# Hybrid neighbourhood-attention layer on one core: another order of the last first-group products, and a place for silu's table load

## The chip, the cores and the metric

One core of a Trainium2 chip runs the whole layer. The metric is the device time of one execution, in microseconds. Before the change it is 590.04 us, the median of 3 runs (589.38 to 590.24).

## What is computed

One layer of a diffusion backbone on 1024 tokens (a grid of 16 rows by 64 columns) of width 1024, with 256 context tokens. Cut to what matters:

```
h  = rmsnorm(x, norm_g) * (1 + scale) + shift          # scale, shift, gate = silu(c) @ w_ada + b_ada
hc = rmsnorm(ctx, norm_g) * (1 + scale_c) + shift_c
q, k, v, za, u, bg, cg, zc = split(h @ w_in)           # 8 parts of 512 columns
kc, vc = split(hc @ w_in[:, 512:1536])
attn = neighbourhood_attention(norm(q), norm(k), v, norm(kc), vc, rpb) * silu(za)
conv = bg * conv3(cg * u) * silu(zc)
out  = x + gate * (concat(attn, conv) @ w_out)
```

All is float32. The kernel splits each operand of a large product into a high and a low part and adds three products: high by high, high by low, low by high.

## The kernel before

The program has four stages. Times in brackets are where they lie in the profile.

**First stage (0 to 63 us).** A list of words, `STEPS` (L37 to L49), sets the order in which the instructions are written; an engine runs its instructions in the order in which they are written, and a wait at one holds all that stand behind it. The stage makes `h` for eight blocks of 128 features, `h0` to `h7`, and at the same time the first group of 384 projected columns: u, bg and cg of the first conv group. That group has six PSUM banks: `acc00`, `acc10`, `acc20` for the first half of the tokens (u, bg, cg) and `acc01`, `acc11`, `acc21` for the second half. A word `fcHKI` (L665) is three products of half H, feature block K: I = 0 is high by high, 1 the weights' low part by `h`'s high part, 2 the weights' high part by `h`'s low part. `qhK` and `qlK` (L673, L679) make the high part (ScalarE) and the low part (VectorE) of the weights of the *next* 384 columns, the tile `w`, out of `wr`, which a DMA has loaded. `conv0` (L756) takes one step of `conv_group(0)` (L409): the first such step copies the first half's u from its bank to `ub` (ScalarE, `keep`, L416) and multiplies it with cg in its bank into `cu` (VectorE, `multiplied`, L420); the second step does the same for the second half. `Rt2` transposes and `R2` copies the context's row scales (`rs2<-tr`). `rg1` to `rg3` are three VectorE products for the rotary table.

**Second stage (63 to about 250 us).** The first pools of PSUM are closed and others opened over the same banks. 32 token tiles are projected (`proj_tile`, L307): each is one PSUM tile `pacc`, 8 feature blocks of 3 products. Its first tile lies in the bank that held `acc00`, its second in that of `acc20`. The products of block K need `w`'s high part K, and from the second on its low part K.

**Third stage (250 to 508 us).** 36 calls of `quarter(n)` (L1022) do the attention, with the exponentials on ScalarE. Between its pieces stand filler products (`pu`), the units of 128 columns of the gates and of the conv groups. A unit has two halves, each with a `pu` tile of its own, and there are two such tiles, so a unit's first half waits until the tile of the unit before it has been read. The last two units are the conv gate zc (read by `silus`, L500: silu out of PSUM into `zs`) and bg. Quarter 34 has the last exponentials. ScalarE needs another function table for silu than for exp; an `ACT_TABLE_LOAD` is put ahead of the first instruction that needs another table than the one loaded.

**Fourth stage (508 us to the end).** The output projection, seven blocked products into `pout` tiles, their scaling and addition, and the stores.

Of the kernel before, what the change touches and what calls it, by code (L numbers as in the profile page):

```python
# [13 lines left out]
AF = mybir.ActivationFunctionType  # L14
# [34 lines left out]
]  # L49
CONTEXT = "Hi0 Hi1 Lo0 Lo1 Hi2 Hi3 Lo2 Lo3 Hi4 Hi5 Lo4 Lo5 Hi6 Hi7 Lo6 Lo7"  # L50

# [4 lines left out]
def body(tc, es, x, xb, xt, cb_, ct, w_mod, w_gate, b_ada, w_grp, w_col, q_g, k_g, bias, w_out, vecs, cst, out):  # L56
# [21 lines left out]
    pe, act, dve, pool = every = [ordered(e) for e in (nc.tensor, nc.scalar, nc.vector, nc.gpsimd)]  # L78
# [49 lines left out]
    few = cp.tile([P, 8], F32, name="few")  # L128
# [5 lines left out]
    ones = oner[:, 0:1]  # L134
# [196 lines left out]
    def do_acts():  # L331
        for c in soon + (slow if not any(c[1] and c[1].__name__ == "product" for c in soon) else []):
            if c[0]:
                c[0]()
                c[0] = None

    def do_frees(most):
        while most > 0 and slow and slow[0][2] is not None and not slow[0][0]:
            slow.pop(0)[1]()
            most -= 1  # L340
        return most

    def do_dves(most=99):
        most = do_frees(most)
        for queue in chores:
            while queue and not queue[0][0] and (queue is soon or most > 0 and not soon):
                on_dve = queue.pop(0)[1]
                if on_dve:
                    on_dve()
                    most -= 1  # L350
# [612 lines left out]
    def pair_of(n):  # L963

        h, g = divmod(n, 4)
        return [(a, heads[h], 2 * g + a) for a in range(2)] if 0 <= h < NH else []

    def both(v, n, part=slice(0, 31)):

        lo, hi = span(2 * (n % 4))  # L970
        return v[:, :, part.start * 12:min(part.stop, hi - lo) * 12]

    def maxima_of(n):

        lo, hi = span(2 * (n % 4))
        v = mg[:]
        return bass.AP(v.tensor, v.offset + lo * 16, [list(v.ap)[0], [4, 2], [16, hi - lo], [1, 12]])
# [6 lines left out]
    def maxima(e):  # L984

        blocks = turned(e) if e < 4 * NH else []
        nb = len(blocks)
        if not blocks:
            return None
        pm = psm.tile([P, 512], F32, name="pmx", tag="C", bufs=2)  # L990
        for i, b in enumerate(blocks):
            pe.transpose(pm[:, i * P:(i + 1) * P], mx[:, b * P:(b + 1) * P], ident)
        rm = ap.tile([P, 2], F32, name="rm", tag="rm", bufs=8)
        dve.tensor_reduce(rm[:, :nb], pm[:, :nb * P].rearrange("p (i k) -> p i k", i=nb), AX.X, ALU.max)

        def back():
            for i in range(nb):
                pe.transpose(pm[:, 256 + i * P:256 + (i + 1) * P], rm[:, i:i + 1].broadcast_to([P, P]), ident)
            v, step = mg[:, blocks[0] * P:], (blocks[-1] - blocks[0]) * P or P
            act.copy(bass.AP(v.tensor, v.offset, [list(v.ap)[0], [step, nb], [1, P]]),  # L1000
                     pm[:, 256:256 + nb * P].rearrange("p (i k) -> p i k", i=nb))
        return back

    def weighted(hd_):

        hd_.po = psm.tile([P, 512], F32, name="po", tag="O", bufs=2)[:]
        sides = [], []
        for m in range(4 * hd_.h, 4 * hd_.h + 4):
            for i, _, j in pair_of(m):
                for piece in hd_.pieces(j, sbs[m][:, i]):  # L1010
                    sides[piece[0]].append(piece[1:])
            for piece in hd_.ctx_pieces(m % 4):
                sides[piece[0]].append(piece[1:])
        for side in sides:
            side.sort(key=lambda piece: -piece[-1].free_size())
        last = len(sides[0]) - 1
        for k in range(last + 1):
            for side in sides:
                j, dst, src = side[k]
                pe.matmul(dst, hd_.v[:, j], src, start=k == 0, stop=k == last, skip_group_check=True)  # L1020

    def quarter(n):  # L1022

        live = lambda m: 0 <= m < 4 * NH
        ticks = TICKS[n]
        e, o = n - 3, n - 4
        left = do_frees(1) + 2 if n > 2 else 3
        if live(o):
            heads[o // 4].ctx_sum(o % 4)
        for m in () if o % 4 == 0 else (o - 1, o) if o % 4 == 3 else (o - 1,):  # L1030
            for i, hd_, j in pair_of(m):
                hd_.lat_sum(j, sbs[m][:, i])
        do_dves(left)
        if gating and next(gating[0], "end"):
            gating.pop(0)
        now = pair_of(n)
        for i, hd_, j in now:
            hd_.scores(j, sbank[:, i])
        if n == 0:
            next(fill)  # L1040
            ticks -= 1
        back = backs.pop() if backs else None
        ctx_now = [m for m in ([0] if n == 0 else [n + 1] if n % 2 else []) if live(m)]

        def between():
            if back:
                back()
            if n:
                next(fill, None)

        for m in ctx_now:
            heads[m // 4].ctx_scores(m % 4, between)
        if back and not ctx_now:
            if not now:
                next(fill, None)
                ticks -= 1
            back()

        def biased():
            sb = sbs[n] = sb_new()  # L1060
            bt = now[0][1].bt[:].rearrange("p v n -> p (v n)")[:, :1128].rearrange("p (a n) -> p a n", a=2)
            for at, slot, w_ in (((0, 31, 8), (8, 15, 16)), ((0, 0, 31),), ((0, 0, 31),), ((0, 0, 15), (15, 39, 8)))[n % 4]:
                dve.tensor_tensor(sb[:, :, at * 12:(at + w_) * 12], sbank[:, :, at * 12:(at + w_) * 12],
                                  bt[:, :, slot * 12:(slot + w_) * 12], ALU.add)

        if now and n >= 2:
            biased()
        if live(e):
            heads[e // 4].ctx_exp(e % 4)
            w = both(sbs[e], e)  # L1070
            w4 = w.rearrange("p a (c r) -> p a c r", r=12)
            dve.tensor_tensor(w4, w4, maxima_of(e), ALU.subtract)
            act.activation(w, w, AF.Exp)
        for _ in range(n > 0 and not ctx_now):
            next(fill, None)
        if 0 < n and n - 2 < 4 * NH:
            backs.append(maxima(n - 2))
        done = []
        if live(o) and o % 4 == 3:
            hd_ = heads[o // 4]  # L1080
            weighted(hd_)
            hd_.total()
            done.append(hd_)
            if hd_.s:
                ready.append(hd_.p)
        if now:
            if n < 2:
                biased()
            for m in ctx_now:
                heads[m // 4].ctx_max(m % 4)  # L1090
            for i, hd_, j in now:
                hd_.lat_max(j, sbs[n][:, i])
        for _ in range(ticks - (n > 0)):
            next(fill, None)
        for hd_ in done:
            hd_.finish()
        do_acts()
# [216 lines left out]
    with sbuf("att") as ap, psum("psb") as psb:  # L1314
        sbank = psb.tile([P, 2, 512], F32, name="pss")
        strict[:] = every
        mx = ap.tile([P, T], F32, name="mx")
        sb_new = lambda: ap.tile([P, 2, 384], F32, name="sb", tag="sb", bufs=8)
        mg = ap.tile([P, T], F32, name="mg")
        heads[0].load_v()  # L1320
        for n in range(len(TICKS)):
            h, g = divmod(n, 4)
            if 0 < h < NH and g == 1:
                heads[h].load_v()
            if h + 1 < NH and g:
                nx = heads[h + 1]
                for load in ((nx.masks, nx.load_q), (nx.load_k,), ())[g - 1]:
                    load()
            place_2 = early_loads(n) if n < 35 else place_2
            quarter(n)  # L1330
            if ready:
                p = ready.pop()
                if p < NPAIR - 1:
                    gating.append(gated(p))
                else:
                    reciprocals = recip(p, ri_last[:, :16])
                    next(reciprocals)
        for step in gating:
            for _ in step:
                do_acts()  # L1340
                do_dves()
        load_y(place_2, 2)
# [256 lines left out]
```

## Time and profile before

| | us |
|---|---|
| median of 3 runs | 590.04 |
| the profiled execution's own time | 589.67 |
| its span, first to last instruction | 587.80 |
| PE (TensorE matmuls) busy | 578.4 |
| DVE (VectorE) busy | 438.9 |
| ACT (ScalarE) busy | 282.2 |
| granted TensorE clock | 1.000 |

A row of the timeline has the start and the length in us, the engine, the line, the operation, what is written and read, the shape and how many such instructions were merged; in brackets stands how long the engine was idle before, and what ended the wait. Most rows have L71, the line of the helper that emits them, so tiles tell the rows apart, not lines. A matmul's length reaches until its result is out; the next one starts before that, so the pitch from start to start is shorter than the length.

### The profile page before, as it was taken

To read this page: it belongs to the slowest core of one execution; us is meant where nothing else is said; L and a number is where in the kernel's file an instruction comes from. 1 tells how busy PE (TensorE), PEld (TensorE's weight loads), DVE (VectorE), ACT (ScalarE), POOL (GpSimd) and SP (SyncE) were. 2 spreads that over 40 slices of the span, in tenths; PEclk is the share of its full clock that TensorE was granted. 3 is DMA by queue.
4 is the path that set the end of the run, shared out by engine and by line. 5 is a ranking of instruction groups with operands and counts; after the bars stand their busy time and mean duration, and the time that the engine had idled before them with its cause. 6 is when DMAs were issued, how large, how long until landed. Compare 5 with 4: busy or idle time off the path is not lost.

```text
span 587.8 us, 9905 instructions
## 1 busy us (share of the span) xinstructions
PE 578.4 (98%) x3532; PEld 483.4 (82%) x3532; DVE 438.9 (75%) x890; ACT 282.2 (48%) x652; POOL 57.4 (10%) x82
## 2 busy tenths in 40 slices
PE   8899999999999999999999999999999999999997
PEld 4578899999999999988878787878787866888886
DVE  1578779755846745367998788998978897999952
ACT  5636355436525546333463464466545646543420
POOL 1001024123123222100000000000000001100000
PEclk9999999999999999999999999999999999999999
DMA  8997576946765786685253647555757273673532
GB/s 327 410 413 268 177 258 188 308 149 219 247 207 186 249 302 233 213 314 200 92 191 129 241 139 224 195 209 160 251 188 254 93 251 114 231 249 88 200 125 90
DMA packets 66678, 126.14 MB, mean 215 GB/s; under 512 B 8713, under 2 KB 27649, under 8 KB 64324
## 3 DMA queue, kind: packets, MB, share of 16 engines
q1 hardware_dynamic: 66244, 124.70, 60.9%
q0 software_dynamic: 384, 0.81, 0.6%
q8 instruction: 28, 0.46, 0.3%
q14 instruction: 22, 0.18, 0.1%
HBM read 92.38 MB, written 33.10 MB: 213 GB/s over the span
## 4 chain that ended last, share of the span: by engine, by line
PE 89%; DMA 4%; DVE 3%; ACT 2%; issue 1%; SPq 0%; POOL 0%; DVEq 0%; ACTq 0%
PE pu L71 29%; PE pacc L71 22%; PE pout L71 13%; PE acc L71 5%; PE po L71 4%; PE cacc L71 4%; PE pss L71 3%; DMA xn<-in_xb 3%; PE pc L71 3%; PE pmx L71 2%; PE trA L71 1%; PE tr L71 1%; DMA y_d<-tb 1%; PE trB L71 1%; ACT sqj L71 1%
## 5 line engine op out<-in xcount | busy, mean ns | idle before, releaser
L71 PE MATMUL pu<-h,uh 128*128 128x512 f32 x544 | 174.6, 402 | 0.5 <-ACT zs L71 0.5
L71 PE MATMUL pacc<-w,h 128*128 128x384 f32 x768 | 138.9, 337 | 1.1 <-ACT ub L71 0.6
L71 PEld LDWEIGHTS pacc<-w,h 128*128 128x128 f32 x768 | 132.7, 188 | 1.9 <-ACT ub L71 1.1
L71 PEld LDWEIGHTS pu<-h,uh 128*128 128x128 f32 x544 | 97.3, 188 | 19.3 <-issue 1.2
L71 PE MATMUL pu<-h,ul 128*128 128x512 f32 x272 | 106.5, 392 | 0.0
L71 PE MATMUL pout<-right,left 128*128 128x512 f32 (+2 forms) x348 | 77.0, 383 | 0.0
L71 PEld LDWEIGHTS pout<-right,left 128*128 128x128 f32 x348 | 64.4, 188 | 12.7
L71 PEld LDWEIGHTS pu<-h,ul 128*128 128x128 f32 x272 | 51.1, 188 | 11.5
L71 POOL TENSOR_TENSOR ss<-ss,few 128x4 f32<-128x4 f32 (+1 forms) x40 | 41.4, 1035 | 126.7 <-DVE ss L71 126.4
L71 ACT COPY sc<-pc 128x512 f32<-128x512 f32 x32 | 18.7, 587 | 44.8 <-PE pc L71 44.8
L71 ACT ACTIVATE sc<-sc 128x512 f32<-128x512 f32 x32 | 20.3, 633 | 34.3 <-DVE sc L71 34.1
L71 PE MATMUL acc<-h,w 128*128 128x512 f32 x144 | 35.3, 397 | 1.4 <-ACT h L71 1.4
L71 ACT ACTIVATE sq<-pacc 128x256 f32<-128x256 f32 x32 | 12.4, 387 | 47.0 <-PE pacc L71 46.3
L71 DVE TENSOR_TENSOR sum<-sum,sb 128x372 f32<-128x372 f32 (+2 forms) x64 | 31.1, 486 | 2.8
L71 DVE SCALAR_TENSOR_TENSOR m<-pout,ab,m 128x512 f32<-128x512 f32 (+2 forms) x34 | 22.9, 717 | 13.2 <-PE pout L71 13.1
L71 PEld LDWEIGHTS acc<-h,w 128*128 128x128 f32 x144 | 26.3, 188 | 7.8 <-ACT h L71 2.1
L71 ACT ACTIVATE qn<-pacc,ss 128x64 f32<-128x64 f32 x128 | 30.0, 330 | 4.9 <-PE trA L71 2.5
L71 DVE TENSOR_TENSOR mx<-mx,sb 128x372 f32<-128x372 f32 (+2 forms) x64 | 30.8, 482 | 1.4
L71 DVE TENSOR_REDUCE ss<-sq 128x4 f32<-128x260 f32 (+1 forms) x40 | 15.7, 393 | 21.6 <-ACT sq L71 21.5
L71 DVE TENSOR_TENSOR ul<-uraw,uh 128x512 fp32r<-128x512 f32 x34 | 23.1, 686 | 9.4 <-ACT uh L71 9.4
L71 DVE TENSOR_TENSOR sb<-pss,bt 128x192 f32<-128x192 f32 (+3 forms) x48 | 27.6, 602 | 2.5 <-PE pss L71 2.5
L71 DVE TENSOR_TENSOR sb<-sb,mg 128x744 f32<-128x744 f32 (+2 forms) x32 | 26.6, 833 | 0.0
(142 smaller groups left out, 848.6 us busy)
## 6 DMA issues: line engine op xcount, KB each, us to landing
uraw<-in_w_col SPq DMA_DIRECT2D x34, 256.0 KB, 4.2
slab<-in_w_mod SPq DMA_DIRECT2D x8, 1024.0 KB, 8.9
q_d<-qs SPq DMA_DIRECT2D x32, 256.0 KB, 4.3
k_s<-k_d SPq DMA_DIRECT2D x8, 1024.0 KB, 7.3
q_s<-q_d SPq DMA_DIRECT2D x16, 512.0 KB, 3.7
wr<-in_w_grp SPq DMA_DIRECT2D x40, 192.0 KB, 5.0
bt<-in_rpb SPq DMA_DIRECT2D x8, 564.0 KB, 7.2
xn<-in_xb SPq DMA_DIRECT2D x8, 512.0 KB
```

Of the source, the lines that this page charges most:

```text
L71: i = emit(*a, **kw)
```

## The change

In the word list the two halves of the last feature block (K = 7) change places: before, each of the three kinds of product is done for the first half and then for the second (`fc070`, `fc170`, `fc071`, `fc171`, `fc072`, `fc172`); now the first half's three come first, then the second half's three. The first `conv0` now stands right behind the first half's last product, ahead of `qh7`, `ql4`, `ql5` and `ql6`; `R2` goes behind the second `conv0`. The second edit adds one ScalarE instruction behind quarter 34: a silu of a [128, 1] constant into an unused column, which brings the table load with it.

```
@@ STEPS
-    "fc070 qh4 lo17 qh5 fc170 qh6 ql2 q7 e0 e1 e2 e3 fc071 qh7 ql3 fc171 R2 ql4 fc072 conv0 ql5 ql6 fc172",
+    "fc070 qh4 lo17 qh5 fc071 qh6 ql2 q7 e0 e1 e2 e3 ql3 fc072 conv0 qh7 fc170 ql4 fc171 ql5 ql6 fc172",
...
@@ the loop over the quarters
             quarter(n)
+            if n == 34:
+                act.activation(few[:, 5:6], ones, AF.Silu)
             if ready:
```

What this does on the engines at three places. In the names, `w_886`, `w_890`, `w_912`, `w_915`, `w_920` and `w_936` (now `w_943`) are the weights of the second stage for the blocks 2 to 7; `ub` and `cu` are the copy and the product of u.

ScalarE at the end of the first stage, before:

```order
L71 CAST w_920<-wr_902 128x384
L71 CAST w_936<-wr_923 128x384
L71 COPY rs2_166<-tr_898 128x256
L71 COPY ub_950<-acc00_155 128x512
L71 COPY ub_958<-acc01_157 128x512
L71 ACTIVATE cv_966<-cu_947,vecT_115 128x512
```

and with the change:

```order
L71 CAST w_920<-wr_902 128x384
L71 COPY ub_940<-acc00_155 128x512
L71 CAST w_943<-wr_923 128x384
L71 COPY ub_957<-acc01_157 128x512
L71 COPY rs2_166<-tr_898 128x256
L71 ACTIVATE cv_966<-cu_937,vecT_115 128x512
```

The copy of the first half's u moved ahead of the cast of block 7's weights, and the copy of the row scales went behind both copies of u.

VectorE at the same place, before:

```order
L71 TENSOR_TENSOR w_890<-wr_782,w_890 128x384
L71 TENSOR_TENSOR w_912<-wr_857,w_912 128x384
L71 TENSOR_TENSOR cu_947<-acc20_156,ub_950 128x2x16x16
L71 TENSOR_TENSOR w_915<-wr_881,w_915 128x384
L71 TENSOR_TENSOR w_920<-wr_902,w_920 128x384
L71 TENSOR_TENSOR cu_947<-acc21_158,ub_958 128x2x16x16
L71 TENSOR_TENSOR rg_866<-rw8_707 128x8x64 x3
L71 TENSOR_TENSOR w_936<-wr_923,w_936 128x384
```

and with the change:

```order
L71 TENSOR_TENSOR w_890<-wr_782,w_890 128x384
L71 TENSOR_TENSOR cu_937<-acc20_156,ub_940 128x2x16x16
L71 TENSOR_TENSOR w_912<-wr_857,w_912 128x384
L71 TENSOR_TENSOR w_915<-wr_881,w_915 128x384
L71 TENSOR_TENSOR w_920<-wr_902,w_920 128x384
L71 TENSOR_TENSOR cu_937<-acc21_158,ub_957 128x2x16x16
L71 TENSOR_TENSOR rg_866<-rw8_707 128x8x64 x3
L71 TENSOR_TENSOR w_943<-wr_923,w_943 128x384
```

One row moved: the first half's product `cu` now stands ahead of the low part of block 4's weights, and three low parts stand between the two products instead of two.

ScalarE in the last quarter of the attention (`sums` and `ob` take the last head's results out of PSUM, `uh` is the high part of the last unit's weights, the two `zs` are the gate's silus), before:

```order
L71 ACTIVATE cv_5526<-cu_5062,vecT_115 128x512
L71 COPY sums_5565<-ptot_5560 128x256
L71 COPY ob_5568<-po_5543 128x512
L71 CAST uh_5572<-uraw_5465 128x512
L71 ACT_TABLE_LOAD
L71 ACTIVATE zs_5607<-pu_5462 128x512
L71 ACTIVATE zs_5609<-pu_5517 128x512
```

and with the change:

```order
L71 ACTIVATE cv_5526<-cu_5062,vecT_115 128x512
L71 ACT_TABLE_LOAD
L71 ACTIVATE few_107<-oner_110 128x1
L71 COPY sums_5566<-ptot_5561 128x256
L71 COPY ob_5569<-po_5544 128x512
L71 CAST uh_5573<-uraw_5465 128x512
L71 ACTIVATE zs_5608<-pu_5462 128x512
L71 ACTIVATE zs_5610<-pu_5517 128x512
```

The table load moved ahead of the three rows that take the last head's results and cast the last weights; one short instruction is new, and the number of table loads stays the same.

More of the change, by code (lines that the diff above doesn't have):

```diff
@@ L1330, in body @@
             quarter(n)
+            if n == 34:
+                act.activation(few[:, 5:6], ones, AF.Silu)
             if ready:
```

4 rows, old and new, of the table STEPS are left out of this document.

## Prediction

> **What bounds the kernel now.** I read the page first: its busy line, and the shares of the chain that ended last. Then the waits of PE from 60 us on, and the timeline around each of them.
>
> ```profile
> PE 578.4 (98%) x3532; PEld 483.4 (82%) x3532; DVE 438.9 (75%) x890; ACT 282.2 (48%) x652; POOL 57.4 (10%) x82
> PE 89%; DMA 4%; DVE 3%; ACT 2%; issue 1%; SPq 0%; POOL 0%; DVEq 0%; ACTq 0%
> ```
>
> PE is the bound: it is idle for 587.8 - 578.4 = 9.4 us. A change can gain little but these, so the question is which of them it touches. PE's waits from 60 us to the end (in total, times, longest, in us) are four:
>
> ```profile
> PE pacc L71 <- ACT ub L71: 0.6, 1, 0.6
> PE pu L71 <- ACT zs L71: 0.5, 1, 0.5
> PE pmx L71 <- DVE rm L71: 0.4, 1, 0.4
> PE pacc L71 <- DVE w L71: 0.4, 1, 0.4
> ```
>
> The change aims at the first two; the fourth is one tile behind the first. I call them A (bank of `acc00` not yet copied), B (low part of block 7's weights not yet there) and C (the gate's tile not yet read). The third is not touched. PE's timeline has A and B like this:
>
> ```profile
> 54.63 3.57 PE L71 MATMUL acc<-h,w 128*128 128x512 f32 x15
> 62.80 0.39 PE L71 MATMUL acc<-h,w 128*128 128x512 f32 x1
> 63.83 4.11 PE L71 MATMUL pacc<-w,h 128*128 128x384 f32 x22 [0.64 <-ACT ub L71]
> 67.61 0.34 PE L71 MATMUL pacc<-w,h 128*128 128x384 f32 x1
> 68.37 8.94 PE L71 MATMUL pacc<-w,h 128*128 128x384 f32 x50 [0.42 <-DVE w L71]
> ```
>
> The idle time in brackets is less than what a wait costs. In the first row 15 products take 3.57 us, and each lasts 0.39, so they start (3.57 - 0.39) / 14 = 0.227 us apart. In the last row the pitch is (8.94 - 0.34) / 49 = 0.1755 us. The result of a product is thus out only after the next one could have started, and the time between these two is lost in a wait without being idle.
>
> **A, priced.** The first stage's last product starts at 62.80, so the next could start at 63.03; it starts at 63.83: 0.80 us. After a wait the stream also starts more slowly: from 63.83 to the 22nd product at 67.61 are 3.78 us, where 21 pitches are 3.69: 0.1. Together **0.9 us**.
>
> **B, priced.** The 23rd product could start at 67.61 + 0.18 = 67.79 and starts at 68.37: 0.58, with the slow restart **0.68 us**.
>
> **Is A gone?** For that the copy of `acc00` must end before 63.03. What ScalarE and VectorE do there, and the issue of the load of block 7's weights:
>
> ```profile
> 59.70 0.33 SPq L71 DMA_DIRECT2D wr<-in_w_grp  x1
> 60.26 0.52 ACT L71 CAST w<-wr 128x384 fp32r<-128x384 f32 x1 [1.20 <-DMA wr<-in_w_grp]
> 62.51 0.51 ACT L71 CAST w<-wr 128x384 fp32r<-128x384 f32 x1 [1.73 <-PE acc L71]
> 62.93 0.36 ACT L71 COPY rs<-tr 128x256 f32<-128x256 f32 x1
> 63.19 1.07 ACT L71 COPY ub<-acc 128x512 f32<-128x512 f32 x2
> 57.75 1.41 DVE L71 SCALAR_TENSOR_TENSOR h<-hw,ab,h 128x512 fp32r<-128x512 f32 x2
> 59.07 1.49 DVE L71 TENSOR_TENSOR w<-wr,w 128x384 fp32r<-128x384 f32 x3
> 63.81 0.69 DVE L71 TENSOR_TENSOR cu<-acc,ub 128x512 f32<-128x512 f32 x1 [3.25 <-ACT ub L71]
> 64.42 1.01 DVE L71 TENSOR_TENSOR w<-wr,w 128x384 fp32r<-128x384 f32 x2
> 65.35 0.69 DVE L71 TENSOR_TENSOR cu<-acc,ub 128x512 f32<-128x512 f32 x1
> 65.95 1.89 DVE L71 TENSOR_TENSOR rg<-rw 128x512 f32<-128x512 f32 x3
> 67.76 0.55 DVE L71 TENSOR_TENSOR w<-wr,w 128x384 fp32r<-128x384 f32 x1
> ```
>
> The last 18 products of the stage are block 7's; the change puts the first half's nine first, so its last starts nine pitches before 62.80, at 60.76, and its result is out at 61.15 (62.80 + 0.39 = 63.19 is when the copy starts now, without delay). Its inputs are there: the low parts of `h7` are made from 57.75 to 59.16. ScalarE is free from 60.78 on, when `qh6` ends, and waits there until 62.51. So the copy runs in that gap, 61.15 to about 61.75. PE needs it at 63.03: 1.3 us to spare. **A goes, 0.9 us.** `qh7` stays where it is, since it waits for its weights: their load is issued at 59.70, and the cast at 62.51 comes 2.8 us later (the row names PE, but the products that read this buffer before were done long ago, so I put it down to the DMA).
>
> **What is late next: B.** PE now reaches the 23rd product at 63.03 + 22 x 0.1755 = 66.89, 0.9 us earlier, and if the last low part stayed at 68.31 all of A would come back as a longer B. It doesn't stay. VectorE's idle 3.25 us before 63.81 waited for the first copy. Now the first `cu` starts at 61.15 + 0.62 = 61.77 (0.62 is the distance from copy to product above), then three low parts, 0.61 and then 0.465 us apart by the rows above, so the second `cu` could start at 63.78. Its copy starts at 63.19 as soon as PE is done, `qh7` being over at 63.02, so the second `cu` starts at 63.81 instead of 65.35. From there to the end of the last low part are 68.31 - 65.35 = 2.96 us: it ends at 66.77. PE needs it at 66.89. **B all but goes**; as the margin is 0.1 us, I take 0.63 of its 0.68, and the bounds are 0.3 (a quarter of a microsecond late and a restart) and 0.68.
>
> The three low parts that now stand behind the first `cu` (blocks 4 to 6) end near 63.9; PE needs block 4's at 63.03 + 13 x 0.1755 = 65.3. `R2` moves from 62.93 to about 63.8: nobody waits, since the scales are read after the conv taps. DMA issues do not move: the `wr` loads wait for low parts 0 to 2, which stay where they were.
>
> **C, priced.** ScalarE, the last attention matmuls on PE, and the first products of the last unit:
>
> ```profile
> 489.68 0.82 ACT L71 ACTIVATE cv<-cu,vecT 128x512 f32<-128x512 f32 x1
> 493.50 0.37 ACT L71 COPY sums<-ptot 128x256 f32<-128x256 f32 x1 [3.00 <-issue]
> 493.77 0.59 ACT L71 COPY ob<-po 128x512 f32<-128x512 f32 x1
> 494.25 0.63 ACT L71 CAST uh<-uraw 128x512 fp32r<-128x512 f32 x1
> 494.90 1.28 ACT L71 ACT_TABLE_LOAD   x1
> 496.19 1.09 ACT L71 ACTIVATE zs<-pu 128x512 f32<-128x512 f32 x2
> 492.75 0.64 PE L71 MATMUL ptot<-sum,onef 128*32 128x256 f32 x8
> 495.95 0.39 PE L71 MATMUL pu<-h,ul 128*128 128x512 f32 x1
> 496.84 0.73 PE L71 MATMUL pu<-h,uh 128*128 128x512 f32 x2 [0.51 <-ACT zs L71]
> L71 ACT ACTIVATE few<-oner x1: 202/202/202, 228.4 to 228.4; 128x1 f32<-128x1 f32 x1
> ```
>
> The next unit could start at 495.95 + 0.227 = 496.18 and starts at 496.84: 0.66, with 0.1 for the restart (its second product comes at 496.84 + 0.73 - 0.40 = 497.17, 0.33 later instead of 0.227) **0.76 us**. The table load stands on ScalarE right between the cast and the first silu. The change puts it, 1.28 us, and the new instruction, 0.20 us by the like one in the last row, into the 3.00 us idle before `sums`, which waits for PE's `ptot`, out at 493.39. So 1.48 us lie under cover, with 1.5 us of it left; without cover `sums`, `ob` and the cast would each be 1.48 us later. The first silu then starts at 494.88 behind the cast and ends at 495.5, ahead of 496.18. The second waits for its half, out at 495.95 + 0.39 = 496.34, and is needed 24 products later. **C goes, 0.76 us.**
>
> **Does the gain reach the end?** From 496.84 on the chain that ended last has only PE:
>
> ```profile
> 496.84 11.17 PE pu L71 x48
> 508.02 76.85 PE pout L71 x348
> ```
>
> No wait stands in these 88 us, and what the output products need (weights and right sides) is made from PE's own progress, so it comes earlier with PE. The same holds between 68 and 484 us, where the four waits above leave none. I count it all.
>
> **A page weighed against the trace.** The rows above lose 0.90 + 0.68 + 0.76 = 2.34 us where the brackets add up to 0.64 + 0.42 + 0.51 = 1.57. The Trainium skill, page "TensorE: Matmul & The Clock Gate", section "Single matmul latency", gives an isolated product (398 + N) / 2.4 ns, and its section "Back-to-back issue gap" N / 2.4 + 2.5 ns from start to start: the difference, 163 ns, would be what each wait costs beyond its idle time. The trace agrees for the wide products (0.39 - 0.227 = 0.163 us). By the page alone the three waits would be worth, as an estimate, 1.57 + 3 x 0.163 = 2.06 us and the time 588.0, between the forecast and the first rival below; the slow restart of 0.1 us is in the trace and not on the page.
>
> **The sum.** 0.90 + 0.63 + 0.76 = 2.29, say 2.3 us. The profiled execution's own time is 589.67 us (span 587.80 and 1.87 around it), so the changed kernel in such an execution would take 587.4. The median of the runs is 0.37 above that execution, so against the median I forecast **587.7 us**, 0.39% less. A measurement of this kernel can tell about 0.2%, 1.18 us, from no change, so faster means below 588.9 and slower above 591.2.
>
> **The rivals.** First, that only the idle time comes back, 1.57 us: 588.5. For it speaks that the profile counts only this as idle; against it that starts, not ends, set a stream's pace. Chance 0.08.
>
> Second, that the last low part does not come earlier, so that B grows by what A saves and only C is left: 590.04 - 0.76 = 589.3. This needs the second copy to be held, by `qh7` ahead of it if its weights land after 62.7; now they are there at 62.51, 0.2 us before it matters. Each tenth beyond costs a tenth, and all of A and B is gone at 1.5 us. Chance 0.05.
>
> Third, that A and B go, and C stays because something fixed in time, such as the last head's sums on their way through DRAM, is then late for the output stage; or that PE meets a new wait anywhere in the 400 us that follow and gives the whole back. That is 588.5 for the first, 589.7 to 590.0 for the second. Against it: the profile shows PE without a wait there, with VectorE busy 75% and ScalarE 48%. Chance 0.08, half on either side of 588.9.
>
> Fourth, slower. The first copy now stands on ScalarE ahead of `qh7`, and the first `cu` on VectorE ahead of three low parts. If the copy is held, they all are. It stands behind `qh6`, whose weights come by the load issued at 57.86:
>
> ```profile
> 57.86 0.33 SPq L71 DMA_DIRECT2D wr<-in_w_grp  x1
> DMA to landing us min/median/max: 2.4/5.0/6.3
> ```
>
> The cast ran at 60.26, so this load took 2.4 us, the least of its kind. At the most, 6.3, it lands at 64.16, the copy starts at 64.68, the first `cu` at 65.30, the second 0.61 + 3 x 0.465 = 2.01 later at 67.31, and the last low part ends at 70.27: PE goes on at 70.3 instead of 68.37, a loss of 1.95, less C's 0.76: 1.2 us slower, 591.2 to 591.3. The last low part ends 5.59 us after such a copy's start, so A and B are lost from a start at 62.7 on, C's 0.76 too from 63.5 on, and the kernel is slower by over 0.2% only from 64.7 on. Nothing ahead of that load moves, so it should land as it did. Chance 0.04.
>
> **How the numbers follow.** The forecast has the remaining 0.75, with a range of its own of 587.0 to 588.3 from B's bounds (0.3 us), the doubt on the restarts (3 x 0.1) and the 0.4 between single runs. Taking in the first rival to 588.5 and half of the third, 588.8 above leaves less than 2 in 10 outside. Faster: 0.75 + 0.08 + 0.04 = 0.87; same: 0.05 + 0.04 = 0.09; slower 0.04; I move 0.01 from the first to each of the others for the scatter of the measurement.
>
> **What would show it.** In the new profile: PE's waits for `ub` and `zs` gone from the list; the wait for `w` gone or 0.1; the first `ub` copy near 61.2 and the second `cu` near 63.8; the table load near 490.5 and the first `zs` near 494.9 less the 1.5 us by which PE is ahead; PE busy nearly the same and the span 585.5. Wrong would be: `w` as a wait of over 0.5 us, or a new wait in the stages behind.

## The result and the profile after

The changed kernel takes 587.20 us (median of 5 runs, 587.02 to 587.34), the kernel before 589.87 us beside it (5 runs, 589.38 to 590.24). The ratio is 0.9956, with a 95% interval of 0.9945 to 0.9966: 0.44% faster, forecast were 0.39%. The profiled execution takes 587.34 us with a span of 585.6, so 2.33 us less than the one before (589.67). Run again beside the last experiments the change has a ratio of 0.9950 (0.9936 to 0.9963).

The busy line, and what is left of PE's waits from 60 us on:

```profile
PE 577.2 (99%) x3531; PEld 483.3 (83%) x3532; DVE 438.6 (75%) x890; ACT 282.0 (48%) x653; POOL 57.4 (10%) x82
```

```profile
PE pmx L71 <- DVE rm L71: 0.4, 1, 0.4
```

Three of the four waits are gone. PE's *busy* time also falls, by 1.2 us, with the same matmuls in the program (one record fewer in the trace). In a dense stream the tail of each product lies under the next one (a wide product lasts 0.39 us at a pitch of 0.227); ahead of a wait it is counted by itself. In the first and the third stretch of the table below, where the waits were, busy time falls by 0.54 and 0.29 us beside the idle time of 1.06 and 0.51: together the 2.40 us by which the two stretches are shorter. The first 58 us, where the change does nothing, have another 0.54 us of busy time less, and the second stretch has 0.19 more; they are no part of the gain.

The first place in the timeline of PE (start, length), then ScalarE and VectorE, to be held against the rows of before in the prediction:

```profile
58.00 0.38 PE L71 MATMUL tr<-ci,sums 128*128 128x128 f32 x2
58.14 5.02 PE L71 MATMUL acc<-h,w 128*128 128x512 f32 x21
63.00 12.67 PE L71 MATMUL pacc<-w,h 128*128 128x384 f32 x72
75.50 5.71 PE L71 MATMUL cacc<-w,hc 128*128 128x512 f32 x32
```

```profile
59.96 0.51 ACT L71 CAST w<-wr 128x384 fp32r<-128x384 f32 x1 [1.24 <-DMA wr<-in_w_grp]
60.70 0.59 ACT L71 COPY ub<-acc 128x512 f32<-128x512 f32 x1 [0.23 <-PE acc L71]
62.40 0.52 ACT L71 CAST w<-wr 128x384 fp32r<-128x384 f32 x1 [1.11 <-DMA wr<-in_w_grp]
62.82 0.58 ACT L71 COPY ub<-acc 128x512 f32<-128x512 f32 x1
61.32 0.69 DVE L71 TENSOR_TENSOR cu<-acc,ub 128x512 f32<-128x512 f32 x1 [1.56 <-ACT ub L71]
63.43 0.69 DVE L71 TENSOR_TENSOR cu<-acc,ub 128x512 f32<-128x512 f32 x1
65.84 0.55 DVE L71 TENSOR_TENSOR w<-wr,w 128x384 fp32r<-128x384 f32 x1
```

The 72 projections of the first three token tiles are one unbroken row, where before there were 22 and then 50 with a hole ahead of each. The cast of block 7's weights now waits for the DMA with nothing behind it that PE needs at once. Both copies start earlier than forecast (60.70 and 62.82, not 61.15 and 63.19); the last low part ends at 65.84 + 0.55 = 66.39, not at 66.77.

The second place, ScalarE and then PE:

```profile
488.24 0.82 ACT L71 ACTIVATE cv<-cu,vecT 128x512 f32<-128x512 f32 x1
489.08 1.28 ACT L71 ACT_TABLE_LOAD   x1
490.37 0.20 ACT L71 ACTIVATE few<-oner 128x1 f32<-128x1 f32 x1
492.05 0.37 ACT L71 COPY sums<-ptot 128x256 f32<-128x256 f32 x1 [1.48 <-issue]
492.80 0.63 ACT L71 CAST uh<-uraw 128x512 fp32r<-128x512 f32 x1
493.32 0.61 ACT L71 ACTIVATE zs<-pu 128x512 f32<-128x512 f32 x1
494.92 0.60 ACT L71 ACTIVATE zs<-pu 128x512 f32<-128x512 f32 x1 [0.99 <-PE pu L71]
494.50 0.39 PE L71 MATMUL pu<-h,ul 128*128 128x512 f32 x1
494.72 0.61 PE L71 MATMUL pu<-h,uh 128*128 128x512 f32 x2
```

The load and the small silu take 1.5 of the 3.0 us that ScalarE was idle ahead of `sums`, the other 1.48 are left. The first silu ends at 493.93, PE needs its bank at 494.72. PE passes from one unit to the next at its pitch, 0.22 us, without a hole.

To read small differences I divide each trace at four points on PE: the transposes of the context's scales (58.00 above), the first `cacc` (75.50), the last head's first weighted sum `po`, and the first `pout`. The last of these I take from the chain that ended last, which begins `pout` when the product before it is out, 0.16 us behind its start, in each of these traces alike. For the kernel before the first three lie here:

```profile
58.04 0.38 PE L71 MATMUL tr<-ci,sums 128*128 128x128 f32 x2
77.14 5.71 PE L71 MATMUL cacc<-w,hc 128*128 128x512 f32 x32
488.75 1.94 PE L71 MATMUL po<-sc,v 128*64 128x512 f32 x8
```

and `pout` at 508.02. The change has `po` at 487.29 and `pout` at 505.76. The first stretch holds A and B, the third holds C, and what comes ahead of the first, which starts up to 1.1 us earlier or later from one profile to another, is left out. Each row of stretches is one profile:

| kernel | first, us | second, us | third, us | ratio to before (95%) |
|---|---|---|---|---|
| before | 19.10 | 411.61 | 19.27 | |
| the change | 17.50 | 411.79 | 18.47 | 0.9956 (0.9945 to 0.9966) |
| e1, word list only | 17.50 | 411.56 | 19.28 | 0.9968 (0.9956 to 0.9980) |
| e2, early silu only | 19.05 | 411.64 | 18.47 | 0.9994 (0.9985 to 1.0002) |
| e3, copy moved, products in the old order | 18.51 | 411.58 | 19.28 | 0.9991 (0.9982 to 1.0000) |
| e4, products in the new order, copy not moved | 18.81 | 411.57 | 19.27 | 1.0001 (0.9992 to 1.0009) |
| e5, as e3, low part ahead of the rotary products | 17.50 | 411.92 | 19.27 | 0.9971 (0.9960 to 0.9982) |
| e6, the low part's move only | 18.40 | 411.56 | 19.28 | 0.9983 (0.9974 to 0.9992) |
| e7, the change, silu later | 17.67 | 411.57 | 19.37 | 0.9968 (0.9955 to 0.9981) |
| e8, the change and a filler piece moved | 17.50 | 410.89 | 19.04 | 0.9951 (0.9937 to 0.9965) |
| e9, as e8, conv taps moved | 17.50 | 410.95 | 18.47 | 0.9941 (0.9929 to 0.9954) |
| e10, the change again | 17.76 | 411.87 | 18.47 | 0.9950 (0.9936 to 0.9963) |

### The profile page after: what moved, and what is told of

The parts are those of the page before. It is cut to its first block, busy times and chain, and to the rows that moved or that the text cites. A ratio compares the mean times of both kernels' runs of the same rounds, so it can differ in the third digit from the quotient of the medians.

```text
span 585.6 us, 9903 instructions
## 1 busy us (share of the span) xinstructions
PE 577.2 (99%) x3531; PEld 483.3 (83%) x3532; DVE 438.6 (75%) x890; ACT 282.0 (48%) x653; POOL 57.4 (10%) x82
## 4 chain that ended last, share of the span: by engine, by line
PE 91%; DMA 5%; DVE 2%; ACT 1%; SPq 0%; issue 0%; POOL 0%; DVEq 0%; ACTq 0%
PE pu L71 29%; PE pacc L71 23%; PE pout L71 13%; PE acc L71 5%; PE po L71 5%; PE cacc L71 4%; PE pss L71 3%; DMA xn<-in_xb 3%; PE pc L71 3%; PE pmx L71 2%; PE trA L71 1%; PE tr L71 1%; DMA y_d<-tb 1%; PE ptot L71 1%; PE trB L71 1%; DVE sb L71 0%
## 5 line engine op out<-in xcount | busy, mean ns | idle before, releaser
L71 DVE TENSOR_TENSOR qs<-trA,qs 128x512 fp32r<-128x512 f32 x16 | 11.1, 691 | 21.2 <-ACT qs L71 20.2
```

Source lines behind the costliest of these rows:

```text
L71: i = emit(*a, **kw)
```

## The experiments

The profile after shows the first copy starting 2.5 us earlier, and in the profile before it starts right behind two ScalarE instructions that are none of PE's business: the cast of block 7's weights, which waits for a DMA until 62.51 (its row names PE; the same cast's rows in e4, e10 and the change name the DMA), and the copy of the row scales. So there are two theories of A. **P**, the prediction's: the copy started when its half's products were out, and the new order of the products freed it. **Q**: the copy's bank had long been complete, and the copy was held by what stood ahead of it on ScalarE; the new order *there* freed it. e1 to e4 take the change apart.

**e1, the word list only**

```
-            if n == 34:
-                act.activation(few[:, 5:6], ones, AF.Silu)
```

> The new word list without the early silu. My theory: waits A and B go, C stays: 0.90 + 0.63 to 0.68 = 1.5 to 1.6 us under the kernel before; PE's first pacc near 63.0, no wait for ub or w, the wait for zs still 0.5; the first ub copy near 60.7 as with the whole change. Rival (only idle time comes back): 0.64 + 0.42 = 1.06 us under.

Measured: 588.27 us, 1.57 below 589.84; the first stretch is 17.50, 1.60 less than before, and PE's wait for `zs` stays at 0.5. My price holds, and with 1.60 instead of 1.06 the rival that only idle time comes back is out for A and B.

**e2, the early silu only** (the word list of before)

> The early silu with the old word list. My theory: C alone goes, 0.76 us under the kernel before; the waits for ub (0.6) and w (0.4) stay. Rival (only idle time comes back): 0.51 us under. Second rival (the early PE meets late data at the output): nothing, 0.0.

Measured: 589.36 us, 0.48 below. The times can't tell 0.76 from 0.5, nor from nothing (the interval reaches to 1.0002), but the third stretch can: 18.47 instead of 19.27, 0.80 less. From `pout` to the end are 79.8 us as before, so it is not given back there.

**e3, the copy moved, the products in the old order**

```
-    "fc070 qh4 lo17 qh5 fc170 qh6 ql2 q7 e0 e1 e2 e3 fc071 qh7 ql3 fc171 R2 ql4 fc072 conv0 ql5 ql6 fc172",
+    "fc070 qh4 lo17 qh5 fc170 qh6 ql2 q7 e0 e1 e2 e3 fc071 ql3 fc171 fc072 conv0 qh7 ql4 ql5 ql6 fc172",
```

(and `R2` behind the second `conv0`, so ScalarE and VectorE have the order of the change)

> Old order of the products (halves in turn), new order on ScalarE and VectorE (copy of the first half's u ahead of the cast of block 7's weights, row scales last). No early silu. Theory Q (the copy was late because it stood on ScalarE behind a cast that waited for a DMA until 62.5 and behind the row scales; its own bank was complete at 62.06, since u is the first of the three columns of its last group of products): the copy starts at 62.1, PE's wait for ub goes, the last low part ends at 67.65, and 0.7 us are gained; the wait for w grows from 0.4 to about 0.6. Theory P (as in the prediction, the copy starts when all products of its half are out, here 62.5): the copy starts at 62.5, the last low part ends at 68.1, and 0.2 us are gained.

Measured: 589.28 us, and the first stretch 18.51, 0.59 less than before. PE's `pacc` rows and the copy (this trace is 0.84 us later than the one before at the transposes):

```profile
63.88 4.00 PE L71 MATMUL pacc<-w,h 128*128 128x384 f32 x22
68.59 8.96 PE L71 MATMUL pacc<-w,h 128*128 128x384 f32 x50 [0.71 <-DVE w L71]
```

```profile
62.94 0.59 ACT L71 COPY ub<-acc 128x512 f32<-128x512 f32 x1 [1.79 <-PE acc L71]
63.42 0.52 ACT L71 CAST w<-wr 128x384 fp32r<-128x384 f32 x1
```

62.94 - 0.84 = 62.10: Q's start, not P's 62.5 (e5, with the same two orders, has it at 62.07, with the transposes 0.03 us earlier: 62.10 again). A's wait is gone without any change to the products. B's wait has grown from 0.42 to 0.71, since PE is there earlier and the last low part is not early enough.

**e4, the products in the new order, the copy not moved**

```
-    ... fc170 qh6 ql2 q7 e0 e1 e2 e3 fc071 qh7 ql3 fc171 R2 ql4 fc072 conv0 ql5 ql6 fc172",
+    ... fc071 qh6 ql2 q7 e0 e1 e2 e3 fc072 qh7 ql3 fc170 R2 ql4 fc171 conv0 ql5 ql6 fc172",
```

> New order of the products (first half's three kinds ahead of the second half's), old order on ScalarE and VectorE (cast of block 7's weights and row scales ahead of the copy). No early silu. Theory Q: the copy still waits behind the cast and the row scales and starts at 63.2, so nothing changes: 0.0 us, waits for ub 0.6 and w 0.4 as before. Theory P (the order of the products sets when the copy can start): the copy starts near 61.2, A goes, 0.9 us or more.

Measured: 590.01 us, ratio 1.0001. The copy did not start near 61.2:

```profile
62.21 0.52 ACT L71 CAST w<-wr 128x384 fp32r<-128x384 f32 x1 [1.86 <-DMA wr<-in_w_grp]
62.63 0.36 ACT L71 COPY rs<-tr 128x256 f32<-128x256 f32 x1
62.89 1.08 ACT L71 COPY ub<-acc 128x512 f32<-128x512 f32 x2
```

It stands behind the cast as before, and the cast behind its DMA. In this profile the cast ran 0.30 us earlier than in the one before, and the copy and the first stretch (18.81) moved by just that, 0.30 and 0.29 (PE's wait for `ub` is 0.32 instead of 0.64): the wait A follows the landing of a load, whatever the order of the products. P has fallen. Of the 1.1 us by which the copy was late, the cast has the larger part and the copy of the row scales 0.26 (62.93 to 63.19); e3 takes both out of the way, and no run parts them. What then is the new order of the products for? With the copy moved it makes 17.50 of 18.51: the first copy can run at 60.7 instead of 62.1, and VectorE's chain to the last low part starts earlier. That is a matter of B, and e5 and e6 show that B can be had more simply.

**e5, as e3, and the last low part ahead of the rotary products**

```
-    "conv0 rg1 rg2 rg3 ql7",
+    "conv0 ql7 R2 rg1 rg2 rg3",
```

> Old order of the products, copy ahead of the cast on ScalarE as in the change, and on VectorE the last low part (block 7's weights) ahead of the three rotary products instead of behind them. No early silu. Theory Q (two queues were the cause, ScalarE's for A and VectorE's for B): the last low part ends 1.8 us earlier than in the run with the copy moved alone, PE needs it 0.8 us earlier than it came there, so both A and B go: 1.6 us under the kernel before, as much as the word list of the change, and no wait for ub or w. Rival (the products' order is needed for B): a wait for w of 0.4 us or more stays and at most 0.9 us are gained.

Measured: 588.23 us, first stretch 17.50, no wait for `ub` or `w`. VectorE has the last low part early enough although the first `cu` starts later than with the change:

```profile
62.69 0.69 DVE L71 TENSOR_TENSOR cu<-acc,ub 128x512 f32<-128x512 f32 x1 [3.06 <-ACT ub L71]
64.70 0.68 DVE L71 TENSOR_TENSOR cu<-acc,ub 128x512 f32<-128x512 f32 x1
65.30 0.55 DVE L71 TENSOR_TENSOR w<-wr,w 128x384 fp32r<-128x384 f32 x1
65.77 1.89 DVE L71 TENSOR_TENSOR rg<-rw 128x512 f32<-128x512 f32 x3
```

So the products need not be moved at all; two places in two queues do it.

**e6, the low part's move only**: the last line of e5's diff without `R2`, in the kernel before.

> The kernel before with one word moved: block 7's low part ahead of the three rotary products. Theory: A stays as it is, B goes whole: the wait for w disappears, the wait for ub stays at 0.6 and 0.68 us are gained. Rival (only idle time comes back): 0.42 us.

Measured: 589.00 us, first stretch 18.40, so 0.70 less, and these waits of PE:

```profile
PE pacc L71 <- ACT ub L71: 0.6, 1, 0.6
PE pu L71 <- ACT zs L71: 0.5, 1, 0.5
PE pmx L71 <- DVE rm L71: 0.4, 1, 0.4
```

B by itself is worth 0.70, as priced (0.68), where the list counts 0.4. A and B together are 1.60 (e1), so A is 0.90 by difference.

**e7, the change with the load where ScalarE is not idle**: the small silu stands behind `ob`, ahead of the last cast.

> The whole change, but with silu's short instruction, and so its table load, behind the copy of the last head's output (ob) and ahead of the last cast, where ScalarE is not idle. Theory (the gain of C is the idle time that the load now lies in, not that it comes earlier): the first silu starts 1.5 us later than with the change, PE's wait for zs is back and about 0.2 us longer than before the change: 0.7 us, so the kernel is 0.9 to 1.0 us slower than the whole change, 1.3 us under the kernel before. Rival (any place ahead of the silus does): as fast as the whole change, 2.2 us under.

Measured: 587.98 us, 1.78 below the 589.76 of the kernel before beside it, where 1.3 were expected; by the three stretches it is 1.37 below and 0.85 above the change. The third stretch is 19.37, 0.90 above the change's and 0.10 above the kernel before:

```profile
492.70 1.28 ACT L71 ACT_TABLE_LOAD   x1
494.00 0.20 ACT L71 ACTIVATE few<-oner 128x1 f32<-128x1 f32 x1
494.11 0.60 ACT L71 CAST uh<-uraw 128x512 fp32r<-128x512 f32 x1
494.62 1.08 ACT L71 ACTIVATE zs<-pu 128x512 f32<-128x512 f32 x2
495.26 0.73 PE L71 MATMUL pu<-h,uh 128*128 128x512 f32 x2 [0.60 <-ACT zs L71]
```

The load is the same, it comes earlier than in the kernel before, and C is back. It is the idle time that it lies in, not its place ahead of the silu, that makes the gain.

**e8, a filler piece moved ahead of the last wait of PE**

```
             if not now:
-                next(fill, None)
-                ticks -= 1
+                for _ in range(1 + (n == 34)):
+                    next(fill, None)
+                    ticks -= 1
             back()
```

> The whole change, and in quarter 34 two filler pieces instead of one ahead of the transposes that wait for VectorE's reduced maxima. The only wait that PE has left from 60 us on (pmx for rm, 0.4 us idle, priced like the others at 0.7 us from start to start) should go: PE has 1.4 us of products there and waits 0.6 us. ScalarE's copy of the maxima comes 0.6 us later, but the subtraction that needs it starts 1.4 us behind that copy today. Theory: 0.7 us under the whole change, 2.9 us under the kernel before, no PE wait from 60 us on. Rival: the exponentials come later and the last weighted sums wait for them: no gain against the change, or a new wait of po for sb.

Measured: 586.83 us, ratio 0.9951, no better than the change's. The wait is gone and the second stretch is 410.89, 0.67 below e1's; but the third is 19.04, 0.57 above the change's. PE's weight loads in the weighted sums have a new wait:

```profile
486.77 0.19 PEld L71 LDWEIGHTS po<-sc,v 128*64 128x64 f32 x3 [0.37 <-ACT sc L71]
```

The rival was right: PE comes 0.67 us earlier to exponentials that do not: the first of them starts 410.77 us behind the first `cacc`, against 410.82 in e1. I had looked at the copy of the maxima and not at what VectorE does next: two conv taps, 1.54 us, ahead of the subtraction that the exponentials need.

```profile
483.91 1.54 DVE L71 SCALAR_TENSOR_TENSOR cv<-cu,vecT,cv 128x512 f32<-128x512 f32 x2
485.37 0.68 DVE L71 TENSOR_TENSOR sc<-sc,mg 128x512 f32<-128x512 f32 x1
```

**e9, the taps behind that subtraction**

```
-        do_dves(left)
+        if n != 34:
+            do_dves(left)
...
             act.activation(w, w, AF.Exp)
+        if n == 34:
+            do_dves(left)
```

> As e8, and in quarter 34 VectorE's two conv taps (1.54 us) stand behind the last subtractions instead of ahead of them. Theory (what e8 gave back, 0.4 to 0.5 us, is the last weighted sum waiting for exponentials that stand behind those taps): the last exponentials come 1.4 us earlier, PE's stage of the weighted sums takes 4.0 us again, and the span is 0.5 us under e8's: about 0.6 to 0.7 us under the whole change, 2.9 to 3.0 under the kernel before. Rival (the taps are then late for the gate's product or the output stage): a new wait behind 490 us and no gain against e8.

Measured: 586.71 us, ratio 0.9941 (0.9929 to 0.9954) beside 0.9950 (0.9936 to 0.9963) for the change in the same session. The stretches are 410.95 and 18.47: the gain of e8 stays, and PE has no wait from 60 us to the end. VectorE and ScalarE there:

```profile
484.66 0.69 DVE L71 TENSOR_TENSOR sc<-sc,mg 128x512 f32<-128x512 f32 x1
485.27 0.73 DVE L71 TENSOR_TENSOR sb<-sb,mg 128x552 f32<-128x552 f32 x1
489.13 1.53 DVE L71 SCALAR_TENSOR_TENSOR cv<-cu,vecT,cv 128x512 f32<-128x512 f32 x2
```

It has the lowest median here, 0.49 us under the change's. By the last two stretches it is 0.84 us shorter (410.95 + 18.47 against 411.79 + 18.47), of which about 0.2 is a wait at 441 us that the change's profile has and this one has not (below). The intervals of the two ratios overlap: the trace shows that the fourth wait went, the times alone don't show that this version beats the change.

**e10, the change again**

> The whole change once more, for comparison on the same chip with e9: 2.2 to 2.4 us under the kernel before.

Measured: 587.20 us, against 590.06 for the kernel before in that session, 2.9 us, with a ratio whose interval reaches from 2.2 to 3.8 us. Its first stretch is 17.76, 0.26 more than in the first profile. ScalarE shows why:

```profile
62.72 0.51 ACT L71 CAST w<-wr 128x384 fp32r<-128x384 f32 x1 [1.66 <-DMA wr<-in_w_grp]
63.14 0.58 ACT L71 COPY ub<-acc 128x512 f32<-128x512 f32 x1
```

The transposes ran 0.22 us earlier here (57.78), the load landed 0.3 us later, and the cast held the *second* copy, which the change leaves behind it. That is the prediction's second rival in small; e7 (17.67) has it too.

## Why the prediction was right, and where its reasons failed

**What bounds the kernel.** Right: PE, and the four waits. The gain came from three of them, and in e9's profile the fourth is gone too.

**The price of a wait.** Right. 0.90, 0.68 and 0.76 were forecast from start to start; measured are 0.90 (1.60 less 0.70), 0.70 (e6) and 0.80 (e2 and the change). The rival that only idle time comes back would have had 0.64, 0.42 and 0.51. The stretches add up to 2.40 for the three, the tenth of a microsecond or so per wait by which PE's stream restarts slowly included. By the Trainium skill, page "TensorE: Matmul & The Clock Gate" (sections "Single matmul latency" and "Back-to-back issue gap"), latency less gap, the prediction's estimate was 2.06 us; what the traces have above it is about those three tenths.

**A: the size right, the reason wrong.** The step that failed is "62.80 + 0.39 = 63.19 is when the copy starts now, without delay". The two times agree by chance: 62.80 is the start of the stage's last product, and that belongs to the second half. u is the first of the three columns in each group of products, so the bank of its first half was complete at 61.67 + 0.39 = 62.06 (block 7's 18 products have a pitch of 0.227, and the last one that u's bank needs is the 13th), 1.1 us before the copy. The copy stood behind a cast that waited for a DMA until 62.51 and behind the row scales. I had read the cast's wait, and its place in the order was in my own listing, but I asked only whether ScalarE would be free at the new time, not what had held it at the old one. e4 shows that the step as I put it gives nothing, e3 that the queue does. The new time was off for the same reason: in the new order u's bank needs the first 7 of the 18 and is out at 60.30 + 0.39 = 60.69, and the copy ran at 60.70, not at 61.15. That A's price came back all the same is luck, since the same edit that reordered the products also moved the copy ahead of the cast.

**B: right, for a margin that was luck.** By my sum the last low part would end 0.1 us before PE needs it, and in the first profile it had 0.5: the second copy could start right behind the cast, at 62.82, since it needs only u's bank and not the half's last product. In e10, where the load landed later, 0.26 us of B came back; the 0.44 that were left lie inside the bounds of 0.3 and 0.68 that I set.

**C: right** in size, cover and what is left of it (1.48 us forecast as 1.5). Measured are 0.80 for 0.76, and e7 shows what it costs without the cover.

**Does the gain reach the end?** Nearly. The change's second stretch is 411.79 and 411.87 in its two profiles and 411.92 in e5, against 411.56 to 411.64 in before, e1 to e4, e6 and e7. All three have a wait at one pair of context scores at 441 us that the others have not: PE's weight load waits 0.34, 0.39 and 0.21 us for ScalarE's copy of the pair before. In the change's first profile it accounts for the excess:

```profile
441.28 0.30 PEld L71 LDWEIGHTS pc<-q_s,kc_s 128*128 128x128 f32 x2 [0.34 <-ACT sc L71]
```

In e5 a second wait of 0.3 us stands beside it. What makes it come in some profiles and not in others I have not settled: e7 has the word list and the extra silu without it. The 0.2 to 0.3 us are within the forecast's range.

**The sum.** Forecast 2.3 us; the profiled executions differ by 2.33, the medians by 2.67 with an interval from 2.0 to 3.2. In such an execution 587.4 were forecast and 587.34 measured; the median, 587.20, is 0.5 under the 587.7 forecast, since the profiled execution before lay 0.37 under the 590.04 that I forecast against, and the one after 0.14 above it.

## What to carry to other kernels

When an engine waits for a copy, find what stood ahead of that copy on its own engine at the old time; the data may have been ready for long, and two times that agree to a hundredth prove nothing. Price a wait of TensorE from the start of the last product to the start of the second one behind it, not by its idle time: here 0.42 to 0.64 idle cost 0.70 to 0.90. The table load was free in ScalarE's idle time and gained nothing where ScalarE was busy. A wait that is removed by moving the bound engine forward was won here only when what it needs next was moved too, as e8 and e9 show.

## What the runs showed of the hardware

After a wait of half a microsecond the first matmuls come more slowly: in the profile before the second started 0.28 and 0.27 us behind the first at 128x384 (A and B), where the pitch is 0.1755, and 0.34 at 128x512 (C) with a pitch of 0.227, with the granted clock at 1.00 all the time. The load of 192 KB on which A hung was there 2.81 us after its issue in the profile before (59.70 to the cast at 62.51) and 3.35 us after it in e10 (59.37 to 62.72); the other eight profiles in which the cast waits for it lie between. Half a microsecond of scatter in one load is not far below the 0.70 to 0.90 us of a wait here, and it shows in single profiles (e4, e7, e10) before it shows in medians.
